# A hybrid S5, mLSTM and Conformer trunk on one core: low parts and layer-norm rows from GpSimd to VectorE

## The chip, the cores and the metric

The kernel runs on one core of a Trainium2 chip. Five engines work beside one another: TensorE (PE in the profile, PEld its weight loads), VectorE (DVE), ScalarE (ACT), GpSimd (POOL) and SyncE (SP). The time is that of one execution in device microseconds; of several runs the median is taken.

## What is computed

Four layers over 256 latent tokens and 256 context tokens, 1024 channels, in float32. Layers 0 and 3 mix tokens by an S5 state space layer, layer 1 by an mLSTM, layer 2 by a Conformer convolution. After each mixer comes a feed-forward with a 3x3 depthwise convolution on the token grid. Every sub-layer ends in a layer norm over the residual:

```python
for i in range(DEPTH):                       # 4; kinds 0, 1, 2, 0
    u = h * (1 + scale1) + shift1            # from c (latent) or c_ctx (context)
    y = mixer[kind](u)
    h = layer_norm(ALPHA * h + (1 + g1) * y, post_ln_g[i, 0], post_ln_b[i, 0])
    f = conv_ffn(h * (1 + scale2) + shift2)  # (gelu(dwconv(u @ w_gate)) * (u @ w_up)) @ w_down
    h = layer_norm(ALPHA * h + (1 + g2) * f, post_ln_g[i, 1], post_ln_b[i, 1])
# layer_norm(x, g, b) = (x - mean) * rsqrt(var + eps) * g + b; the context stream stops before the end of layer 3
```

The output is the latent stream after layer 3, whose feed-forward (the last) is computed for the latent tokens alone. FFN_HIDDEN is 2816, that is 22 units of 128 channels.

## The kernel before

**Products.** A float32 product is made of three matmuls of a 32-bit type with a shorter mantissa: each factor is split into a high part (a copy into that type) and a low part (the factor less its high part), and `mm3` (L186 to L190) issues high times high, high times low and low times high. `split` (L160) has ScalarE write the high part and `lo` (L155) subtracts: on VectorE where `e` is "V", on GpSimd where it is "G". For weights (`wload`, tile `whl`, 128 x 1024 twice) the engine is taken from `self.lo_pat`, "V" almost everywhere; ahead of the last feed-forward it is set to "VG", every second weight on GpSimd (L1859).

**Stages.** S5 (layer 0), feed-forward 0, mLSTM, feed-forward 1, Conformer, feed-forward 2 (with the context half of the last S5 layer worked into its end), the rest of that S5 layer (`s5_last`), and the last feed-forward. A feed-forward (`ffn`) makes units 0 to 11 of its hidden layer, a first part of the product with w_down, units 12 to 21, and the rest. A unit f has two weights and the products pg and pu over 512 columns (256 in the last); `ffn_act` copies pg, runs the nine taps of the depthwise convolution on it (the middle one on ScalarE, the others at L505 on VectorE), GELU, the product with pu (L520), and splits the result into `hid` with e="G" (L522). The mLSTM splits its 16 blocks `xc` with "G" for the first 15 (`self.gv`, L656).

**The join of two stages.** A stage ends with its tail products and `close`. Per token block t (0 to 3, of 128 tokens) the residual is added to z, `norm` makes the statistics (`stats`, with a power operation on GpSimd at L351) and z becomes the normed block without gain and bias. `next_x` transposes z by TensorE (tile `ut`), applies gain, bias, scale and shift by column, and splits the result into the next stage's operand X. The same z is also needed as h, by rows, for the next residual: `post` multiplies it by the row of gains and adds the row of biases, both halves of 512 columns, on GpSimd (L419, L420), and stores the result `hh` to DRAM from GpSimd's queue (L421). `close` calls it as the blocks come, and in feed-forward 2 `posts` is called from inside the S5 scan of `s5_last` for t = 2 and 3. In the last feed-forward the block t = 3 goes through `norm_out` (L353) instead, two fused instructions on VectorE, and is stored from SyncE; t = 2 is normed and posted.

**Slots.** `f5` tiles (512 columns; `gate`, `conv`, `hh`, `ytmp` and others) share a ring of 8, the large `h` slots (X, hid, the gain and bias rows of `rows`, the Conformer's hx, its diagonals `dg` and its accumulator `cvo`) a ring of 6. In the Conformer, TensorE does 12 to 15 of the 31 taps as products with diagonals that ScalarE writes (L552), and VectorE the others at L580.

The framework orders the instructions of each engine itself, by its own estimate of times, within what the data and the slots allow; what the code issues first has precedence only so far.

Of the kernel before, what the change touches and what calls it, by code (L numbers as in the profile page):

```python
# [13 lines left out]
ALU = mybir.AluOpType  # L14
# [10 lines left out]
G = 64  # L25
# [27 lines left out]
class Trunk:  # L53
    def __init__(self, ctx, tc, A, out):
        self.tc, self.nc, self.A, self.out = tc, tc.nc, A, out
        ep = lambda **k: ctx.enter_context(tc.tile_pool(**k))
        self.cp = ep(name="cp", bufs=1)
        self.wp = ep(name="wp", bufs=4)
        self.zp = ep(name="zp", bufs=4)
        self.sp = ep(name="sp", bufs=2)  # L60
        self.hp = ep(name="hp", bufs=1)
        self.dp = ep(name="dp", bufs=1, space=bass.MemoryType.DRAM)
        self.pm = ep(name="pm", bufs=4, space=bass.MemoryType.PSUM)
        self.pa = ep(name="pa", bufs=4, space=bass.MemoryType.PSUM)
        nc = self.nc
        c = self.cp.tile([P, 560], F32, name="consts")
        nc.sync.dma_start(c, A["consts"])
        self.ident = c[:, 0:128]
        self.tri = (c[:, 128:256], c[:, 256:384])
        self.foldi, self.foldf = c[0:32, 384:392], c[0:32, 392:400]  # L70
        self.diag16 = c[:, 400:416]
        self.gmask = c[:, 416:424]
        self.rep = c[:, 424:552]
        self.sgn = c[:, 552:553]
        self.dmask = c[0:8, 553:555]
        self.half = c[:, 555:556]
        self.lncol = self.cp.tile([P, 2 * DEPTH, 2, KD], F32, name="lncol")
        nc.sync.dma_start(self.lncol, A["lncol"])
        self.mods = {}
        cc = self.cp.tile([P, KD, 2], F32, name="ccin")  # L80
        nc.sync.dma_start(cc, A["cc"])
        self.cs = self.cp.tile([P, KD, 32], F32, name="cs")
        nc.vector.memset(self.cs, 0.0)
        nc.scalar.activation(self.cs[:, :, 0:2], cc, AF.Silu)
        self.fillers = deque()
        self.load = {"V": 0.0, "G": 0.0}
        self.lo_n = 0
        self.lo_pat = "V"
        self.last_w = None
        self.nxr = 3  # L90
        self.gv = 15
        self.npe = (12, 12, 12, 12, 12, 12, 14, 15)
        self.nw, self.hold = 0, None
        self.hf, self.hm, self.hcv = (4, 4), (1, 2), (2, 4)
        self.last_mm = None
        self.final = False
        self.plan = (0, 0, 0, 0, 0, 0, 0, 0, 1, 0)
        self.norm_e = "ASAS"
        self.nkb = 4
        self.nrp, self.ngt, self.nr0, self.nr1, self.nr2 = 5, 5, 4, 0, (2, 2, 0, 0)  # L100
        self.nrq = 4
        self.nlate = 2
        self.nmid = 1
        self.pre = self.mm
        self.nf0, self.nf1, self.nf2 = 2, 4, 1
# [130 lines left out]
    def close(self, tts, mms, emit, end, X=None):  # L236
        R, z, hdst, nxt = end
        if nxt and X is None:
            X = nxt["begin"]()
        pend, outs = None, []  # L240
        for t in tts:
            r = mms(t)
            if pend is not None:
                nxt["pair"](pend, z, X)
                pend = None
            emit(t, r)
            if self.final and t == 3:
                self.norm_out(R, z[t], hdst(t))
                continue
            self.norm(z[t], z[t], D, self.norm_e[t])  # L250
            outs.append(t)
            if t in (1, 3):
                if nxt:
                    pend = t // 2
            if t == 2:
                while len(outs) > (0 if self.final else 1):
                    self.post(R, z, outs.pop(0), hdst)
        if pend is not None:
            nxt["pair"](pend, z, X)
        with ExitStack() as st:  # L260
            if len(tts) == 2:
                st.enter_context(self.tc.issue_after(self.last_pow.ins))
            for t in outs:
                self.post(R, z, t, hdst)
        return X

    def mod_units(self, l, order=(1, 0, 2, 4, 3, 5), ring=("w32", W32), late=False):
        nc, A = self.nc, self.A
# [140 lines left out]
        else:  # L409
            nc.vector.tensor_tensor(out=z[t][:, hs], in0=z[t][:, hs], in1=tmp, op=ALU.add)  # L410

    def post(self, R, z, t, dst):
        nc = self.nc
        if dst(t) is None:
            return
        for half in range(2):
            hs = slice(half * 512, half * 512 + 512)
            hh = self.f5("hh")
            nc.gpsimd.tensor_tensor(out=hh, in0=z[t][:, hs], in1=R["lng"][:, hs], op=ALU.mult)  # L419
            nc.gpsimd.tensor_tensor(out=hh, in0=hh, in1=R["lnb"][:, hs], op=ALU.add)  # L420
            (nc.sync if self.final else nc.gpsimd).dma_start(dst(t)[:, hs], hh)  # L421

    def hdram(self, name):
        h = self.dp.tile([4, P, D], F32, name=name)
# [2 lines left out]
    def ffn(self, l, X, tts, hsrc, hdst, pool, nxt, mid=None):  # L427
        nc, A = self.nc, self.A
        lat = 0 not in tts
        spans = [(256, 512)] if lat else [(0, 512)]  # L430
        a0 = 256 if lat else 0
# [3 lines left out]
        z = {t: self.zt(f"z{t}") for t in tts}  # L435
        hid = {}

        def gu(fs, stag=False):
            if stag and not lat:
                outs = []  # L440
                for f in fs:
                    for j, nm in ((0, "pg"), (1, "pu")):
                        outs.append((self.mm(nm), [self.wload(A["fgu"][l, f, j])]))
                self.dense(outs, X, [(0, 256), (256, 512)])
                for i, f in enumerate(fs):
                    hid[f] = self.ffn_act(cw[:, f], outs[2 * i][0], outs[2 * i + 1][0], a0, hact)
                return
            for f in fs:
                pg, pu = self.mm("pg"), self.mm("pu")
                self.dense([(pg, [self.wload(A["fgu"][l, f, 0])])], X, spans)  # L450
                self.dense([(pu, [self.wload(A["fgu"][l, f, 1])])], X, spans)
                hid[f] = self.ffn_act(cw[:, f], pg, pu, a0, hact)
                self.fill(-(-len(self.fillers) // (NF - f)) if l == 0 else pool["fill"])

        def part(f0, f1, first, ts=tts, hook=None):
# [34 lines left out]

        def posts():
            for t in (2, 3):
                self.post(R, z, t, hdst)

        return (posts, steps), z

    def ffn_act(self, w, pg, pu, a0, hact):
        nc = self.nc
        g = self.f5("gate")
        nc.scalar.copy(g[:, a0:], pg[:, a0:])  # L500
        c = self.f5("conv")
        nc.scalar.activation(c[:, a0:], pg[:, a0:], AF.Identity, scale=w[:, 4:5], bias=w[:, 9:10])  # L502

        def tap(out, src, i):
            nc.vector.scalar_tensor_tensor(out=out, in0=src, scalar=w[:, i:i + 1], in1=out, op0=ALU.mult, op1=ALU.add)  # L505

        if a0 == 0:
            tap(c[:, 1:256], g[:, 0:255], 3)
            tap(c[:, 0:255], g[:, 1:256], 5)
        cl = c[:, 256:512].rearrange("p (r w) -> p r w", r=4)  # L510
        gl = g[:, 256:512].rearrange("p (r w) -> p r w", r=4)
        for dy in (-1, 0, 1):
            for dx in (-1, 0, 1):
                if dy == 0 and dx == 0:
                    continue
                r0, r1 = max(0, -dy), 4 - max(0, dy)
                c0, c1 = max(0, -dx), 64 - max(0, dx)
                tap(cl[:, r0:r1, c0:c1], gl[:, r0 + dy:r1 + dy, c0 + dx:c1 + dx], (dy + 1) * 3 + dx + 1)
        nc.scalar.activation(g[:, a0:], c[:, a0:], AF.Gelu_apprx_tanh)
        nc.vector.tensor_tensor(out=c[:, a0:], in0=pu[:, a0:], in1=g[:, a0:], op=ALU.mult)  # L520
        x = hact()
        self.split(c[:, a0:], x[:, 0, a0:], x[:, 1, a0:], e="G")  # L522
        return x

    def conformer(self, l, X, hsrc, hdst, pool, nxt):
# [61 lines left out]
        for i0 in range(0, KD, 1):  # L587
            dgs = diags(i0)
            outs = [(self.mm(n), [self.wload(A["cvin"][i0, j])]) for j, n in ((0, "pa"), (1, "pg"))]
            self.dense(outs, X, [(0, 256), (256, 512)] if i0 == 0 else [(0, 512)])  # L590
            late.append((i0, *glu(i0, outs[0][0], outs[1][0]), dgs))
            if i0:
                cv.append(conv(*late.pop(0)))
            self.fill(pool["cf"])
        cv.append(conv(*late.pop(0)))
        self.lo_pat = "V"
# [34 lines left out]
    def mlstm(self, l, X, hsrc, hdst, pool, nxt):  # L631
# [21 lines left out]
        def finish(i, c):  # L653
            nc.scalar.activation(c, c, AF.Silu)
            x = cact()
            self.split(c, x[:, 0], x[:, 1], e="G" if i < self.gv else "V")  # L656
            xc.append(x)
            bb = f5("bb")
            nc.scalar.activation(bb, c, AF.Copy, scale=hc[:, i, 1:2])
# [2 lines left out]
        for i in range(KE):  # L662
# [12 lines left out]
            if late:  # L675
                late.pop()()
            late.append(lambda i=i, c=c: finish(i, c))
            self.fill(pool["fill"])
        late.pop()()
        wg = self.zt("wg")[:, 0:3 * KE * 16].rearrange("p (w e n) -> p w e n", w=3, e=KE)  # L680
# [1157 lines left out]
    def run(self):  # L1838
# [17 lines left out]
        h6 = lambda t: hs[6](t) if t >= 2 else None  # L1856
        late, z = self.ffn(2, X, range(4), hs[5], h6, pool, None, lambda z: self.s5_part(prep, CTX, z))
        X, z = self.s5_last(prep, z, late, hs[6], hs[7], nx(3, 1, 6), m3[pool["m3"]:])
        self.lo_pat = "VG"  # L1859
        self.final = True  # L1860
        self.ffn(3, X, lat, hs[7], hs[8], pool, None)

# [82 lines left out]
```

## Time and profile before

| what | value |
|---|---|
| median of 3 runs | 3317.68 us (3315.51 to 3320.33) |
| profiled execution, its own time | 3317.72 us |
| span in the trace | 3315.9 us |
| mean granted clock of TensorE | 0.953 |
| busy: TensorE, VectorE, ScalarE, GpSimd | 91%, 65%, 37%, 16% |
| chain that ended last: TensorE, VectorE, DMA | 71%, 11%, 4% |

The page of the profile gives busy times of each engine, shares of the chain of work that ended last, and the costliest groups of instructions with the idle time before them. A share over the whole span hides that the stages have different limits, so the windows of one stage are read beside it: how long each engine was busy in that stretch, and the granted clock of TensorE as a share of full speed.

### The profile page before, as it was taken

The numbers are of one execution on the slowest core, as the hardware profiler recorded it, in microseconds if no ns is written. First come the engines' busy times: TensorE is split into PE (matmuls) and PEld (weight loads), VectorE is DVE, ScalarE is ACT, GpSimd is POOL, SyncE is SP. The second block draws the span as 40 slices with busy tenths as digits, with TensorE's granted clock in tenths as the row PEclk, the third lists the DMA queues.
The fourth block names the chain that finished last, engine by engine and source line by source line (L and its number), as shares of the span: only waits on it lengthen the run. The fifth ranks groups of instructions, "written<-read, shape, count | busy, mean of one in ns | idle before, by whom it ended". The sixth has DMA issues, their size and how long they took to land.

```text
span 3315.9 us, 44356 instructions
## 1 busy us (share of the span) xinstructions
PE 3013.4 (91%) x17323; PEld 2375.5 (72%) x17323; DVE 2140.8 (65%) x3489; ACT 1238.5 (37%) x2014; POOL 526.6 (16%) x456
## 2 busy tenths in 40 slices
PE   6848899998999999998889999998989999868896
PEld 4526777776777777876567778876768788656785
DVE  7795764557422223897665864667887546586988
ACT  3532432334622223333432432426534323244443
POOL 1100310004200000220000410121013101041554
PEclk9869999998999999999899999999999999988999
DMA  6623345444522223565545343223244432486352
GB/s 245 205 101 133 125 152 173 148 142 156 193 83 95 96 102 130 191 241 184 202 150 195 127 157 115 96 78 133 66 136 153 167 127 95 148 330 231 137 201 96
DMA packets 181014, 500.09 MB, mean 151 GB/s; under 512 B 18436, under 2 KB 28228, under 8 KB 177988
## 3 DMA queue, kind: packets, MB, share of 16 engines
q1 hardware_dynamic: 167748, 458.52, 40.1%
q10 hardware_dynamic: 8064, 21.96, 1.7%
q0 software_dynamic: 4992, 16.78, 1.4%
q8 instruction: 136, 2.23, 0.3%
q14 instruction: 74, 0.61, 0.1%
HBM read 443.71 MB, written 53.48 MB: 150 GB/s over the span
## 4 chain that ended last, share of the span: by engine, by line
PE 71%; DVE 11%; DMA 4%; ACT 2%; issue 2%; POOL 1%; POOLq 0%; SPq 0%; DVEq 0%; ACTq 0%
PE pg L188 4%; PE pg L189 4%; PE pg L190 4%; PE nat L189 4%; PE nat L190 4%; PE nat L188 4%; PE pu L190 4%; PE pu L189 4%; PE pu L188 4%; DVE conv L505 3%; DVE whl L155 2%; PE mlq L189 2%; PE mlk L189 2%; PE mlq L188 2%; PE mlk L188 2%
## 5 line engine op out<-in xcount | busy, mean ns | idle before, releaser
L155 DVE TENSOR_TENSOR whl<-w,whl 128x1024 fp32r<-128x1024 f32 x441 | 558.6, 1268 | 536.1 <-ACT whl L160 518.5
L160 ACT CAST whl<-w 128x1024 fp32r<-128x1024 f32 x474 | 493.7, 1048 | 817.4 <-PE nat L190 250.0
L505 DVE SCALAR_TENSOR_TENSOR conv<-gate,cw,conv 128x255 f32<-128x255 f32 (+3 forms) x836 | 402.1, 507 | 136.6 <-ACT conv L502 124.5
L188 PE MATMUL pg<-X,whl 128*128 128x512 f32 (+1 forms) x824 | 300.1, 365 | 17.8 <-DVE conv L520 15.3
L189 PE MATMUL pg<-X,whl 128*128 128x512 f32 (+1 forms) x824 | 296.1, 360 | 14.8 <-DVE X L155 14.3
L190 PE MATMUL pg<-X,whl 128*128 128x512 f32 (+1 forms) x824 | 294.7, 358 | 0.0
L188 PE MATMUL pu<-X,whl 128*128 128x512 f32 (+1 forms) x752 | 268.3, 357 | 4.3 <-DVE conv L520 3.7
L189 PE MATMUL pu<-X,whl 128*128 128x512 f32 (+1 forms) x752 | 268.2, 357 | 0.0
L190 PE MATMUL pu<-X,whl 128*128 128x512 f32 (+1 forms) x752 | 267.9, 356 | 0.0
L155 POOL TENSOR_TENSOR hid<-conv,hid 128x512 fp32r<-128x512 f32 (+1 forms) x88 | 112.9, 1284 | 939.6 <-ACT hid L160 881.8
L189 PE MATMUL nat<-whl,hid 128*128 128x512 f32 x520 | 206.7, 397 | 4.7 <-DVE whl L155 4.7
L188 PE MATMUL nat<-whl,hid 128*128 128x512 f32 x520 | 206.3, 398 | 0.0
L190 PE MATMUL nat<-whl,hid 128*128 128x512 f32 x520 | 204.9, 397 | 0.0
L188 PEld LDWEIGHTS pg<-X,whl 128*128 128x128 f32 x824 | 157.3, 191 | 54.9 <-DVE conv L520 18.1
L283 PE MATMUL mod<-w,cs 128*32 128x256 f32 x1536 | 131.2, 439 | 62.8 <-DMA w<-in_modw 62.6
L189 PEld LDWEIGHTS pg<-X,whl 128*128 128x128 f32 x824 | 156.8, 191 | 41.6 <-DVE X L155 17.2
L190 PEld LDWEIGHTS pg<-X,whl 128*128 128x128 f32 x824 | 157.3, 191 | 24.6
L351 POOL TENSOR_TENSOR mv<-mv,consts 128x1 f32<-128x1 f32 x48 | 29.4, 628 | 854.3 <-DVE mv L350 573.7
L188 PEld LDWEIGHTS pu<-X,whl 128*128 128x128 f32 x752 | 143.8, 191 | 27.3 <-DVE conv L520 3.9
L189 PEld LDWEIGHTS pu<-X,whl 128*128 128x128 f32 x752 | 143.8, 191 | 22.0
L190 PEld LDWEIGHTS pu<-X,whl 128*128 128x128 f32 x752 | 143.7, 191 | 22.0
L283 PEld LDWEIGHTS mod<-w,cs 128*32 128x32 f32 x1536 | 43.2, 117 | 126.0 <-DMA w<-in_modw 70.8
(431 smaller groups left out, 6572.7 us busy)
## 6 DMA issues: line engine op xcount, KB each, us to landing
w<-in_modw SPq DMA_DIRECT2D x192, 512.0 KB, 5.1
w<-in_fgu SPq DMA_DIRECT2D x176, 512.0 KB, 3.8
w<-in_fdn SPq DMA_DIRECT2D x98, 512.0 KB, 3.7
w<-in_glu SPq DMA_DIRECT2D x32, 512.0 KB, 4.8
w<-in_mlup SPq DMA_DIRECT2D x32, 512.0 KB, 3.8
w<-in_mlq SPq DMA_DIRECT2D x32, 512.0 KB, 3.4
w<-in_mlk SPq DMA_DIRECT2D x32, 512.0 KB, 3.5
w<-in_mlv SPq DMA_DIRECT2D x32, 512.0 KB, 3.6
```

The costliest lines, as they stand in the source:

```text
L155: (self.nc.vector if e == "V" else self.nc.gpsimd).tensor_tensor(out=out, in0=src, in1=rd(hi), op=ALU.subtract)
L160: nc.scalar.copy(hi, src)
L188: mm(ps, wh, xh, start=first, stop=False)
L189: mm(ps, wh, xl, start=False, stop=False)
L190: self.last_mm = mm(ps, wl, xh, start=False, stop=last)
L283: nc.tensor.matmul(ps[32 * q:32 * q + 32, 0:256], self.cs[:, k, :], w[:, q * 256:(q + 1) * 256], start=(k == 0), stop=(k == KD - 1), skip_ ...
L351: self.last_pow = nc.gpsimd.tensor_tensor(out=mv[:, 2:3], in0=mv[:, 1:2], in1=self.half, op=ALU.pow)
L505: nc.vector.scalar_tensor_tensor(out=out, in0=src, scalar=w[:, i:i + 1], in1=out, op0=ALU.mult, op1=ALU.add)
```

## The change

Four parts, all between GpSimd and VectorE:

- The low parts of `hid` in all feed-forwards (88, of which 66 over 512 columns) and of the 15 blocks `xc` go to VectorE, and the weights' low parts of the last feed-forward (33 of 66) too.
- `post` works one half at a time and on VectorE; the store stays on GpSimd's queue.
- `close` no longer posts. It puts the halves into a queue, `self.posts`, and the following stage takes two out after each unit, from unit 3 of a feed-forward or of the mLSTM and from block 2 of the Conformer on. z and the rows of gains and biases stay in their slots until then. The four posts inside the S5 scan stay where they are, on VectorE.
- In the last feed-forward both token blocks go through `norm_out`.

```diff
@@ close
-            if self.final and t == 3:
+            if self.final:
                 self.norm_out(R, z[t], hdst(t))
                 continue
             self.norm(z[t], z[t], D, self.norm_e[t])
...
-            if t == 2:
-                while len(outs) > (0 if self.final else 1):
-                    self.post(R, z, outs.pop(0), hdst)
         if pend is not None:
             nxt["pair"](pend, z, X)
-        with ExitStack() as st:
-            if len(tts) == 2:
-                st.enter_context(self.tc.issue_after(self.last_pow.ins))
-            for t in outs:
-                self.post(R, z, t, hdst)
+        self.posts.extend(lambda t=t, half=half: self.post(R, z, t, hdst, half) for t in outs for half in range(2) if hdst(t) is not None)
         return X
+
+    def late_posts(self, n):
+        for _ in range(min(n, len(self.posts))):
+            self.posts.popleft()()
@@ post
-            nc.gpsimd.tensor_tensor(out=hh, in0=z[t][:, hs], in1=R["lng"][:, hs], op=ALU.mult)
-            nc.gpsimd.tensor_tensor(out=hh, in0=hh, in1=R["lnb"][:, hs], op=ALU.add)
-            (nc.sync if self.final else nc.gpsimd).dma_start(dst(t)[:, hs], hh)
+    def post(self, R, z, t, dst, half):
+        V = self.nc.vector
+        hs = slice(half * 512, half * 512 + 512)
+        hh = self.f5("hh")
+        V.tensor_tensor(out=hh, in0=z[t][:, hs], in1=R["lng"][:, hs], op=ALU.mult)
+        V.tensor_tensor(out=hh, in0=hh, in1=R["lnb"][:, hs], op=ALU.add)
+        self.nc.gpsimd.dma_start(dst(t)[:, hs], hh)
@@ ffn, one unit
                 hid[f] = self.ffn_act(cw[:, f], pg, pu, a0, hact)
+                self.late_posts(2 if f > 2 else 0)
@@ ffn_act
-        self.split(c[:, a0:], x[:, 0, a0:], x[:, 1, a0:], e="G")
+        self.split(c[:, a0:], x[:, 0, a0:], x[:, 1, a0:], e="V")
@@ conformer, one block
+            self.late_posts(2 if i0 > 1 else 0)
@@ mlstm
-            self.split(c, x[:, 0], x[:, 1], e="G" if i < self.gv else "V")
+            self.split(c, x[:, 0], x[:, 1], e="V")
...
+            self.late_posts(2 if i > 2 else 0)
@@ run
-        self.lo_pat = "VG"
         self.final = True
```

GpSimd at the first join, from S5 into feed-forward 0, before (z_2729 and z_2730 are the first two token blocks, h_87 the stored rows):

```order
L351 TENSOR_TENSOR mv<-mv,consts 128x1
L419 TENSOR_TENSOR hh<-z_2729,rows 128x512 x2
L420 TENSOR_TENSOR hh<-hh,rows 128x512
L351 TENSOR_TENSOR mv<-mv,consts 128x1
L420 TENSOR_TENSOR hh<-hh,rows 128x512
L421 DMA h_87<-hh 128x512
L351 TENSOR_TENSOR mv<-mv,consts 128x1
L419 TENSOR_TENSOR hh<-z_2730,rows 128x512 x2
L421 DMA h_87<-hh 128x512
```

and now:

```order
L348 TENSOR_TENSOR mv<-mv,consts 128x1 x4
L415 DMA h_87<-hh 128x512 x8
L348 TENSOR_TENSOR mv<-mv,consts 128x1 x4
L415 DMA h_88<-hh 128x512 x6
```

The multiplies and adds are gone from between the power operations (mv), and GpSimd has the stores alone.

VectorE at the start of the Conformer, before (hm a block's gated values, hx its split, cvo the accumulator of its taps):

```order
L560 SCALAR_TENSOR_TENSOR hm<-pa,cvb,sg 128x512
L155 TENSOR_TENSOR whl<-w_17396,whl 128x1024
L155 TENSOR_TENSOR whl<-w_17402,whl 128x1024
L155 TENSOR_TENSOR hx<-hm,hx 128x512
L580 SCALAR_TENSOR_TENSOR cvo<-hm,cvw,cvo 128x2x255
L580 SCALAR_TENSOR_TENSOR cvo<-hm,cvw,cvo 128x2x254 x2
L560 SCALAR_TENSOR_TENSOR hm<-pa,cvb,sg 128x512
L580 SCALAR_TENSOR_TENSOR cvo<-hm,cvw,cvo 128x2x253 x2
L580 SCALAR_TENSOR_TENSOR cvo<-hm,cvw,cvo 128x2x252
L580 SCALAR_TENSOR_TENSOR cvo<-hm,cvw,cvo 128x2x251
L155 TENSOR_TENSOR whl<-w_17557,whl 128x1024
```

and now (z_14016 is the first token block of feed-forward 1):

```order
L155 TENSOR_TENSOR whl<-w_17541,whl 128x1024
L155 TENSOR_TENSOR hx<-hm,hx 128x512
L155 TENSOR_TENSOR whl<-w_17547,whl 128x1024
L556 SCALAR_TENSOR_TENSOR hm<-pa,cvb,sg 128x512
L413 TENSOR_TENSOR hh<-z_14016,rows 128x512 x2
L155 TENSOR_TENSOR whl<-w_17711,whl 128x1024
L414 TENSOR_TENSOR hh<-hh,rows 128x512
L155 TENSOR_TENSOR hx<-hm,hx 128x512
L414 TENSOR_TENSOR hh<-hh,rows 128x512
L576 SCALAR_TENSOR_TENSOR cvo<-hm,cvw,cvo 128x2x255 x3
L576 SCALAR_TENSOR_TENSOR cvo<-hm,cvw,cvo 128x2x254 x6
L576 SCALAR_TENSOR_TENSOR cvo<-hm,cvw,cvo 128x2x253 x6
```

The first taps stood behind the first block's hx; now they stand behind the third one's and the first half-rows of the norm, and those of three blocks come together.

VectorE in the second run of units of the last feed-forward, before:

```order
L520 TENSOR_TENSOR conv<-pu,gate 128x256
L505 SCALAR_TENSOR_TENSOR conv<-gate,cw,conv 128x4x63 x2
L505 SCALAR_TENSOR_TENSOR conv<-gate,cw,conv 128x3x63
L155 TENSOR_TENSOR whl<-w_25545,whl 128x1024
L505 SCALAR_TENSOR_TENSOR conv<-gate,cw,conv 128x192
L505 SCALAR_TENSOR_TENSOR conv<-gate,cw,conv 128x3x63 x2
L505 SCALAR_TENSOR_TENSOR conv<-gate,cw,conv 128x192
L505 SCALAR_TENSOR_TENSOR conv<-gate,cw,conv 128x3x63
L520 TENSOR_TENSOR conv<-pu,gate 128x256
```

and now:

```order
L516 TENSOR_TENSOR conv<-pu,gate 128x256
L155 TENSOR_TENSOR whl<-w_25570,whl 128x1024
L501 SCALAR_TENSOR_TENSOR conv<-gate,cw,conv 128x192
L501 SCALAR_TENSOR_TENSOR conv<-gate,cw,conv 128x4x63
L155 TENSOR_TENSOR hid<-conv,hid 128x256
L501 SCALAR_TENSOR_TENSOR conv<-gate,cw,conv 128x3x63 x3
L155 TENSOR_TENSOR whl<-w_25587,whl 128x1024
L501 SCALAR_TENSOR_TENSOR conv<-gate,cw,conv 128x192
L516 TENSOR_TENSOR conv<-pu,gate 128x256
L501 SCALAR_TENSOR_TENSOR conv<-gate,cw,conv 128x192
L155 TENSOR_TENSOR whl<-w_25604,whl 128x1024
```

Of the weights every one is now there, where it was every second, and each unit's hid has come in; taps of two units are mixed.

## Rows read from the trace of the kernel before

**Rows 1.** the page: an engine, busy us, share of span, instructions
```profile
PE 3013.4 (91%) x17323; PEld 2375.5 (72%) x17323; DVE 2140.8 (65%) x3489; ACT 1238.5 (37%) x2014; POOL 526.6 (16%) x456
```

**Rows 2.** GpSimd groups by shape: xcount, busy us, mean ns, idle
```profile
L155 POOL TENSOR_TENSOR hid<-conv,hid 128x512 fp32r<-128x512 f32 x66 | 92.2, 1399 | 875.0 <-ACT hid L160 817.2 <-issue 57.8
L155 POOL TENSOR_TENSOR whl<-w,whl 128x1024 fp32r<-128x1024 f32 x33 | 89.1, 2703 | 99.5 <-ACT whl L160 99.4
L419 POOL TENSOR_TENSOR hh<-z,rows 128x512 f32<-128x512 f32 x50 | 72.5, 1470 | 21.3 <-ACT z L375 17.0 <-ACT z L371 3.9 <-DVE z L372 0.4
L420 POOL TENSOR_TENSOR hh<-hh,rows 128x512 f32<-128x512 f32 x50 | 72.2, 1461 | 0.1
L351 POOL TENSOR_TENSOR mv<-mv,consts 128x1 f32<-128x1 f32 x48 | 29.4, 628 | 854.3 <-DVE mv L350 573.7 <-DMA hr<-in_x 253.6 <-DVE den L916 26.9
...
L155 POOL TENSOR_TENSOR xc<-xcv,xc 128x512 fp32r<-128x512 f32 x15 | 20.7, 1379 | 63.7 <-ACT xc L160 63.7
```

**Rows 3.** windows: us, busy PE, PEld, DVE, ACT, POOL, granted clock, DMA, GB/s
```profile
2062.00:2174.00 112.00, 112.00 (x482) 89.96 (x481) 71.87 (x133) 43.80 (x58) 11.61 (x9) 1.00 0.29 98
2306.00:2400.00 94.00, 93.81 (x437) 74.71 (x436) 85.56 (x129) 49.84 (x141) 0.00 (x0) 1.00 0.21 68
2400.00:2421.00 21.00, 21.00 (x106) 16.88 (x105) 13.43 (x17) 7.92 (x14) 0.00 (x0) 1.00 0.38 126
3077.80:3163.40 85.60, 73.75 (x579) 71.98 (x578) 81.28 (x110) 41.20 (x72) 47.39 (x30) 0.95 0.43 152
3199.50:3266.10 66.60, 58.01 (x482) 56.76 (x481) 62.36 (x85) 29.81 (x51) 33.29 (x17) 1.00 0.47 162
```

**Rows 4.** windows of the six joins: the second, and the sum of all six
```profile
764.00:812.00 48.00, 33.04 (x145) 25.74 (x144) 40.30 (x60) 19.29 (x32) 30.04 (x27) 0.75 0.41 151
...
sum 243.00, PE 186.53 PEld 156.04 DVE 206.89 ACT 110.45 POOL 166.29; mean PE 31.09 PEld 26.01 DVE 34.48 ACT 18.41 POOL 27.71
```

**Rows 5.** timeline of the second join, two engines: start us, us, instruction
```profile
797.79 4.77 DVE L155 TENSOR_TENSOR X<-u,X 128x256 fp32r<-128x256 f32 x2
...
799.46 2.48 POOL L420 TENSOR_TENSOR hh<-hh,rows 128x512 f32<-128x512 f32 x2
```

**Rows 6.** X as a group; tiles X, z: ns min/median/max
```profile
L155 DVE TENSOR_TENSOR X<-u,X 128x256 fp32r<-128x256 f32 x88 | 70.9, 819 | 13.1 <-ACT X L336 6.9 <-ACT X L339 5.2
...
L155 DVE TENSOR_TENSOR X<-u,X x88: 410/426/4432, 375.4 to 3086.6; 128x256 fp32r<-128x256 f32 x88
...
L372 DVE TENSOR_SCALAR z<-z,mv x12: 535/1497/1508, 369.3 to 3074.8; 128x512 f32<-128x512 f32 x12
```

**Rows 7.** waits of TensorE: us in total, times, longest
```profile
PE ut L330 <- ACT z L371: 14.6, 3, 6.8
PE pg L189 <- DVE X L155: 14.3, 9, 2.8
```

**Rows 8.** VectorE groups, window 2062:2174 (no rows on GpSimd)
```profile
L155 DVE TENSOR_TENSOR whl<-w,whl 128x1024 fp32r<-128x1024 f32 x20 | 24.4, 1220 | 4.1 <-ACT whl L160 3.6 <-DMA w<-in_fgu 0.4
...
L408 DVE SCALAR_TENSOR_TENSOR z<-hr,ytmp 128x512 f32<-128x512 f32 x4 | 2.6, 686 | 1.0 <-DMA hr<-h 1.0
```

**Rows 9.** the taps of the conformer: ns min/median/max of one
```profile
L580 DVE SCALAR_TENSOR_TENSOR cvo<-hm,cvw,cvo x139: 705/731/751, 2283.2 to 2425.3; 128x506 f32<-128x506 f32 x16, 128x502 f32<-128x502 f32 x16, 128x498 f32<-128x498 f32 x16, 128x494 f32<-128x494 f32 x16
```

**Rows 10.** timeline of the S5 scan in layer 3, GpSimd and VectorE
```profile
2943.93 5.26 POOL L419 TENSOR_TENSOR hh<-z,rows 128x512 f32<-128x512 f32 x4
...
2945.46 1.35 DVE L1273 TENSOR_TENSOR sy<-ST,apw 128x128 f32<-128x128 f32 x1
...
2954.81 0.28 DVE L1273 TENSOR_TENSOR sy<-ST,apw 128x128 f32<-128x128 f32 x1
```

**Rows 11.** groups of VectorE by shape, seven units of the last feed-forward
```profile
L505 DVE SCALAR_TENSOR_TENSOR conv<-gate,cw,conv 128x192 f32<-128x192 f32 x15 | 23.3, 1555 | 0.2
```

**Rows 12.** timeline of ScalarE ahead of the conformer
```profile
2259.84 3.90 ACT L552 ACTIVATE dg<-consts,cvws 128x128 fp32r<-128x128 f32 x13
```

**Rows 13.** DMA issues: xcount, KB each, median us from issue to landing
```profile
h<-hh POOLq DMA_DIRECT2D x48, 256.0 KB, 3.0
```

More of the change, by code (lines that the diff above doesn't have):

```diff
@@ L85, in __init__ @@
         self.fillers = deque()
+        self.posts = deque()
         self.load = {"V": 0.0, "G": 0.0}
@@ L90, in __init__ @@
         self.nxr = 3
-        self.gv = 15
         self.npe = (12, 12, 12, 12, 12, 12, 14, 15)
@@ L410, in resid @@
             nc.vector.tensor_tensor(out=z[t][:, hs], in0=z[t][:, hs], in1=tmp, op=ALU.add)
[L412 to L418, printed above, removed]
-            nc.gpsimd.tensor_tensor(out=hh, in0=z[t][:, hs], in1=R["lng"][:, hs], op=ALU.mult)
-            nc.gpsimd.tensor_tensor(out=hh, in0=hh, in1=R["lnb"][:, hs], op=ALU.add)
-            (nc.sync if self.final else nc.gpsimd).dma_start(dst(t)[:, hs], hh)
+    def post(self, R, z, t, dst, half):
[5 more added lines that the diff above has]
+        self.nc.gpsimd.dma_start(dst(t)[:, hs], hh)
     def hdram(self, name):
@@ L492, in posts @@
             for t in (2, 3):
-                self.post(R, z, t, hdst)
+                for half in range(2):
+                    self.post(R, z, t, hdst, half)
         return (posts, steps), z
```

## The prediction

> **What bounds the kernel now.** I read the busy totals first: TensorE works 91% of the span [rows 1], so a gain has to come out of its 302 idle us (3315.9 − 3013.4), and only where VectorE or GpSimd makes it wait. Next the groups of GpSimd, which price what the change touches [rows 2]: of its work, 92.2 + 89.1 + 72.5 + 72.2 + 20.7 = 347 us are low parts and the row multiply and add that move (22 narrower low parts move besides). Then three windows, to see what TensorE does beside that work. In a feed-forward of layers 0 to 2 it has no gap (112.00 of 112.00 us) while VectorE is busy 71.87: that stretch is bound by TensorE [rows 3]. In the last feed-forward it is busy 73.75 of 85.60 and 58.01 of 66.60 us, with VectorE at 81.28 and 62.36: bound by VectorE. At the six joins where one stage's layer norm feeds the next stage's first product, TensorE works 186.53 of 243.00 us and GpSimd 166.29 [rows 4]: 56.5 us of idle TensorE, beside a GpSimd that does hardly anything but the rows of the norm.
>
> What these two have to do with each other is in the timeline of one join [rows 5]: two low parts of X take VectorE 4.77 us while GpSimd's multiply and add run; over the kernel the same instruction takes 410 ns at least, 426 at the median, 4432 at worst, and 70.9 us for 88 in all where 88 × 0.426 is 37.5 [rows 6]. So VectorE's instructions with two operands in SBUF stretch until GpSimd's instruction beside them ends. TensorE waits there for just these: 14.6 us for the normed z, 14.3 us for X in front of the first products [rows 7].
>
> **The parts of the change.** The sum is made against the profiled execution, 3317.72 us (span 3315.9 and 1.8 around it); the median of the three runs, 3317.68, is the same number.
>
> *Rows at the joins, removed.* Each of the first five joins has 16 instructions of 1.47 us on GpSimd (8 halves, a multiply and an add), the sixth 8: 88 of the 100. Without them a join still holds its own chain: statistics already made, the power operation on GpSimd (0.63 us [rows 2]) with the small instructions around it, z at 0.54 us, a transpose, u, and X at 0.43 us [rows 6]; I estimate 3.4 us, for six joins 20. 56.5 − 20 = 36 us gained. As bounds: 12 if only a third of the idle time is due to GpSimd (the first rival), 45 if the chain itself shrinks to 2 us. I take 36: the stretch of the X low parts alone is 70.9 − 37.5 = 33 us, and that of the 12 halves of z up to 12 × (1.50 − 0.54) = 11 [rows 6], and these follow one another. Where the granted clock drops in a join (0.75 in the mean of the second [rows 4], so partly at the lower of its two levels, 1.2 of 2.4 GHz), a shorter gap gives back some of the slow products after it: 4 us for all six, between 0 and 8.
>
> *The same rows, added later on VectorE.* They go into units 3 to 6 of the following stage, two halves per unit, so 4 instructions of 0.69 us (the price of a two-operand instruction of that size without GpSimd [rows 8]): 2.74 us a unit. In a feed-forward a unit takes 11.2 us of TensorE (112 us for 10 units, 20 weights [rows 3, 8]) and 7.2 of VectorE; with 2.74 and the unit's own low part of 0.69 VectorE is at 10.6, below 11.2. So the first three feed-forwards pay nothing: their cover is 0.6 us a unit; if it is gone, four units cost some 1 us each, at most 4 for a stage. The 66 wide low parts and the 15 of the mLSTM [rows 2] hide in the same way, 0.69 us in a unit. The stores stay on GpSimd's queue, which now has little else: they cost no path, since the first reader of h comes a stage part later.
>
> *The conformer pays.* There VectorE is busy 85.56 of 94.00 us beside a TensorE almost without gaps, and 13.43 of the next 21 [rows 3]. Added are 16 instructions of 0.69 us, 11 us. And they hold the slot of the gain rows, of six in that ring, until they are done, so the accumulator of the taps takes a slot only when the first diagonals are used up: in the order on VectorE the taps of the first three channel blocks stand behind the third block's low part. Counted there, about 22 taps of 0.73 us [rows 9] are postponed by that, 16 us. Of these 27 us some 14 fit into what VectorE has free there (8.4 and 7.6 us, less what waits leave unusable); 13 come out at the end of the taps, on which the conformer's transposes wait. Bounds: 0 if the free time takes all of it, 27 if none. I take 12.5.
>
> *The scan of the S5 layer* (layer 3). Before, four multiplies of 5.26 us in all on GpSimd, and four adds behind them, hold VectorE's scan: the same instruction takes 1.35 us beside them and 0.28 after [rows 10]. Of 2 × 5.26 us the scan so loses 1 − 0.28/1.35, 8.3 us; now 8 instructions of 0.69, 5.5 us, stand in it. Gain 3; bounds 0 and 5.
>
> *The last feed-forward.* VectorE per unit after the change: eight taps of 189 to 252 columns, the product and the low part of hid, ten instructions that I price like X's of 256 columns, 10 × 0.43 [rows 6], and two weight low parts of 1.22 [rows 8]: 6.7 us. Before, a unit takes 85.60/12 = 7.1 us in the first run of units [rows 3], and in the second some 7.3 where it is steady, since each weight low part of 2.70 us on GpSimd [rows 2] stretches a tap beside it, to 1.56 us in the mean of one form [rows 11]. TensorE needs 58.01/10 = 5.8 [rows 3], so VectorE stays the bound. The first run of 12 units wins 12 × 0.4 to 0.6 = 5 to 7 and pays 5.5 for the 8 rows instructions that now stand in it: I take 1.5. The second, of 10 units, wins about 0.5 each: 5. The tail loses a GpSimd low part of 2.70 from its chain, and at the very end four instructions of 1.47 us on GpSimd [rows 2] no longer run beside the last norm: 2 each. Sum 10.5; bounds 4 and 18.
>
> **Sum.** −36 − 4 + 0 + 12.5 − 3 − 10.5 = −41, and 1.5 to pay in the four covered stages: −39.5, that is 3317.7 − 39.5 = 3278 us.
>
> **The rivals.**
>
> *A, the joins are their own chain.* GpSimd's rows run beside a norm whose parts follow one another anyway; only a third of the 56.5 us comes back, and the stretched instructions were not those that TensorE waited for. For it: part of TensorE's wait at joins is for ScalarE's z. Against it: 4.77 us for two X low parts of 0.43 is in the chain itself. −12 − 2 + 12.5 + 1.5 − 3 − 10.5 = −13.5: 3304 us.
>
> *B, slower: the conformer runs out of slots.* With the gain rows held through four blocks, the diagonals have one slot only: ScalarE's 24 to 32 diagonal writes of a block, 13 in 3.90 us before [rows 12], so up to 9.6 us for 32, can't start until TensorE has used up the previous block's. Exposed in each of the five blocks up to the last of the rows, that is 48 us, and with 16 for the postponed taps 64, against 52 of all gains less the cover: 3330 us. It decides once the conformer loses more than those 52. Against it: VectorE's and TensorE's orders still have three blocks in flight before the taps begin.
>
> *C, slower: stores starve.* Each store of h waits for GpSimd to hand it out; before, a store landed 3.0 us after it was issued [rows 13], with a VectorE that was itself stopped half the time. If the stores wait for pauses in a VectorE that is now busier, the 8 half-row buffers fill, and the row multiply, on VectorE, stops taps and weight low parts behind it: 24 pairs × 3.0 us = 72 us against the 39.5: 3350 us. The Trainium skill has a rule of this kind ("SBUF — State Buffer", the box on the "DVE blocks DMA" trap in it): transfers issued from GpSimd's queue have their descriptors written by GpSimd, which a VectorE instruction in a two-port mode locks out; the same page, section "Who interferes with whom", says that two-operand instructions don't enter these modes. By the first sentence the time would be that of this rival, by the second that of the forecast. The trace before has its stores at 3.0 us beside such two-operand instructions, so I give it little.
>
> *D, the change does less than it says*: the scheduler may place the postponed rows where it likes. The order shows them in the units named, so no chance of its own.
>
> **How the numbers follow.** A change under 0.2% (6.6 us) can't be told from none here. The forecast has 0.79, A 0.13, B 0.06, C 0.02. The forecast's own bounds: with most terms near their better ends, joins 45, clock 7, conformer 5, scan 4, last 14, it gives −65 (3253); with joins 28, clock 2, conformer 20, scan 0, last 6 it gives −16 (3302). With A inside, the range is 3253 to 3306. A's own spread of some 8 us reaches over the 0.2% line, so 0.05 of it counts as the same; B and C are the slower cases: faster 0.87, same 0.05, slower 0.08.
>
> **What would show it.** Right: the six joins, the same windows, with GpSimd under 1 us each and TensorE idle some 20 us in all; X low parts with a mean near 430 ns; z at 540. Feed-forwards of layers 0 to 2 as long as before per unit (11.2 us). The conformer longer by about 12 us, with TensorE idle at its end behind taps. The last feed-forward at 6.7 us a unit with VectorE over 95% busy. Wrong: the joins still idle 40 us or more with waits on ScalarE (A); waits of ScalarE's diagonals on TensorE in each block and conformer +45 (B); stores landing well over 3 us after issue (C).

## The result and the profile after

The changed kernel takes 3235.31 us (median of 4 runs, 3232.15 to 3237.21): 0.9755 of the kernel before, interval 0.9736 to 0.9773. The forecast was 3278 us, its range 3253 to 3306; the time came out 43 us below the forecast. Five other runs of it gave 0.9760 (0.9742 to 0.9778).

The page, busy time and instructions of each engine [rows 1]:

```profile
PE 2990.6 (92%) x17323; PEld 2356.8 (73%) x17323; DVE 2122.8 (66%) x3724; ACT 1238.9 (38%) x2013; POOL 168.3 (5%) x220
```

VectorE executes 235 instructions more than before and is busy 18 us less. The tiles X and z [rows 6] show why: nothing holds their instructions up any more. The three numbers are ns min/median/max:

```profile
L155 DVE TENSOR_TENSOR X<-u,X x88: 374/424/428, 365.6 to 3029.9; 128x256 fp32r<-128x256 f32 x88
...
L369 DVE TENSOR_SCALAR z<-z,mv x12: 496/542/548, 363.5 to 3022.1; 128x512 f32<-128x512 f32 x12
```

No low part of X lasts longer than 428 ns (4432 before). The waits of TensorE for these two [rows 7] fell from 14.6 and 14.3 us to:

```profile
PE ut L327 <- ACT z L368: 6.2, 3, 4.7
...
PE pg L189 <- DVE X L155: 0.6, 2, 0.4
```

To account for the 82.7 us by which the span fell, the traces were cut at the same products in both: five joins (from the last whole tail product to the end of the next stage's first run of units, to the end of the up projection in the mLSTM, to the first run of diagonals in the Conformer), the Conformer, the S5 layer of layer 3, the last feed-forward. The windows before (us, busy PE, PEld, DVE, ACT, POOL, granted clock, DMA share, GB/s; the second and the fifth join, the sum of the five, then the last feed-forward):

```profile
769.30:891.30 122.00, 107.04 (x466) 85.38 (x464) 77.68 (x99) 79.22 (x123) 51.62 (x43) 0.90 0.56 201
...
2481.30:2636.70 155.40, 148.48 (x809) 118.00 (x807) 111.30 (x186) 66.83 (x96) 42.44 (x36) 0.97 0.47 161
sum 664.50, PE 611.28 PEld 487.00 DVE 464.76 ACT 323.50 POOL 205.46; mean PE 122.26 PEld 97.40 DVE 92.95 ACT 64.70 POOL 41.09
...
3068.40:3315.90 247.50, 199.69 (x1336) 181.78 (x1336) 219.08 (x290) 104.53 (x166) 130.29 (x74) 0.94 0.41 144
```

and after, with the third join too:

```profile
754.80:863.10 108.30, 102.95 (x466) 82.74 (x464) 81.59 (x128) 78.67 (x122) 8.78 (x13) 0.97 0.64 225
1803.40:1955.80 152.40, 151.46 (x811) 122.52 (x810) 119.41 (x232) 69.49 (x100) 5.56 (x10) 1.00 0.46 155
...
2444.20:2590.90 146.70, 144.71 (x808) 114.13 (x806) 111.85 (x211) 65.65 (x96) 5.46 (x10) 1.00 0.50 171
sum 612.80, PE 593.52 PEld 473.02 DVE 455.10 ACT 319.74 POOL 28.00; mean PE 118.70 PEld 94.60 DVE 91.02 ACT 63.95 POOL 5.60
...
3015.30:3233.20 217.90, 192.13 (x1337) 178.22 (x1336) 186.85 (x355) 106.21 (x165) 5.76 (x8) 0.95 0.48 163
...
2023.00:2135.00 112.00, 112.00 (x481) 89.97 (x480) 78.09 (x142) 43.81 (x58) 0.00 (x0) 1.00 0.30 99
```

| stretch | before | after | difference |
|---|---|---|---|
| up to the first join | 363.4 | 360.2 | −3.2 (untouched; 356.2 to 363.4 over all runs) |
| five joins | 664.5 | 612.8 | −51.7: idle TensorE 53.2 to 19.3, busy 611.3 to 593.5 |
| Conformer, diagonals to tail | 196.9 | 206.0 | +9.1 |
| layer 3's S5 | 187.7 | 180.3 | −7.4 |
| last feed-forward | 247.5 | 217.9 | −29.6 |
| the rest | 1655.9 | 1656.0 | 0 |

In the last line of the fence stand ten units of feed-forward 1 [rows 3]: 112 us as before, GpSimd at 0. In the second join the same 466 products take 4.1 us less of busy time, at a granted clock of 0.97 instead of 0.90 (means between the two levels, 1.2 and 2.4 GHz). The window of the fourth join holds 264 products after and 271 before, and the Conformer's behind it 898 and 892, so one to two us of these two differences are the cut. Over the other four joins, with the same products in both to within one, idle time falls by 30.2 us (40.2 to 10.0) and busy time by 14.3 (564.5 to 550.2). By the trace's record of the granted clock, TensorE was busy at the lower level for 39.9 us in these four before and for 8.0 after; half of the 31.9 us would be lost at half the clock, an estimate of 15.9 us beside the 14.3 measured. So the clock accounts for the shorter busy time.

### The profile page after: what moved, and what is told of

Same layout as the page of the kernel before. It is cut to its first block, busy times and chain, and to the rows that moved or that the text cites. A ratio compares the mean times of both kernels' runs of the same rounds, so it can differ in the third digit from the quotient of the medians.

```text
span 3233.2 us, 44254 instructions
## 1 busy us (share of the span) xinstructions
PE 2990.6 (92%) x17323; PEld 2356.8 (73%) x17323; DVE 2122.8 (66%) x3724; ACT 1238.9 (38%) x2013; POOL 168.3 (5%) x220
## 4 chain that ended last, share of the span: by engine, by line
PE 79%; DVE 6%; DMA 4%; ACT 1%; issue 1%; POOL 0%; SPq 0%; DVEq 0%; ACTq 0%; POOLq 0%
PE pg L188 5%; PE pg L189 5%; PE pg L190 5%; PE nat L189 5%; PE nat L190 5%; PE nat L188 5%; PE pu L188 4%; PE pu L189 4%; PE pu L190 4%; PE mlq L189 2%; PE mlq L190 2%; PE mlk L190 2%; PE mlk L189 2%; PE mlk L188 2%; PE mlq L188 2%; PE v L188 2%
## 5 line engine op out<-in xcount | busy, mean ns | idle before, releaser
L155 DVE TENSOR_TENSOR whl<-w,whl 128x1024 fp32r<-128x1024 f32 x474 | 578.7, 1223 | 523.3 <-ACT whl L160 507.9
L501 DVE SCALAR_TENSOR_TENSOR conv<-gate,cw,conv 128x255 f32<-128x255 f32 (+3 forms) x836 | 341.6, 437 | 77.1 <-ACT conv L498 67.4
L188 PE MATMUL nat<-whl,hid 128*128 128x512 f32 x520 | 206.0, 398 | 0.0
L188 PEld LDWEIGHTS nat<-whl,hid 128*128 128x128 f32 x520 | 98.0, 189 | 24.2 <-issue 0.8
```

Of the source, the lines that this page charges most:

```text
L155: (self.nc.vector if e == "V" else self.nc.gpsimd).tensor_tensor(out=out, in0=src, in1=rd(hi), op=ALU.subtract)
L188: mm(ps, wh, xh, start=first, stop=False)
```

## The experiments

The theory to start with: a VectorE instruction with two operands in SBUF lasts as long as GpSimd's beside it, so each part gains where it stood. Ratios are to the kernel before, run beside each kernel.

**The parts alone.** Kernel before with three edits:

```diff
-        self.split(c[:, a0:], x[:, 0, a0:], x[:, 1, a0:], e="G")
+        self.split(c[:, a0:], x[:, 0, a0:], x[:, 1, a0:], e="V")
-            self.split(c, x[:, 0], x[:, 1], e="G" if i < self.gv else "V")
+            self.split(c, x[:, 0], x[:, 1], e="V")
-        self.lo_pat = "VG"
```

> The kernel before with the low parts alone moved to VectorE (hid, xc, the weights of the last feed-forward); rows of the norm stay on GpSimd at the stage ends. Theory 1: a VectorE instruction with two operands in SBUF lasts as long as the GpSimd instruction beside it, so each part gains by itself in the stage where it stood; the low parts carry most of the 30 us that the last feed-forward (247.5 to 218 us) lost. Expected 3290 us (3282 to 3298), joins and Conformer as before. Rival: in the last feed-forward VectorE has no room for 33 more weights, and the 30 us came from the rows and the last norm: 3308 us or more.

0.9922 (0.9904 to 0.9939), 3286.3 us. The other half, the changed kernel with these three lines as they were before:

> The changed kernel with all low parts back on GpSimd: rows of the norm on VectorE within the following stage, and the last norm fused, alone. Theory 1: five joins shorter by 52 us in all, Conformer longer by 9, the S5 scan shorter by 7, in units 3 to 6 some stretch of the rows by hid on GpSimd (4): 3319 - 46 = 3273 us (3264 to 3280). Rival: joins need both parts, since hid and xc low parts on GpSimd beside the first units hold VectorE there too: 3290 us or more.

0.9844 (0.9820 to 0.9868), 3259.6 us. The gains add up: 0.78% and 1.56% against 2.45% together, and both rivals fall. The joins are the rows' alone: cut at the same products, the five take 665 us with the low parts alone, as before the change, and 613 with the rows alone. The last feed-forward, with the low parts alone:

```profile
3064.60:3283.50 218.90, 191.46 (x1336) 176.54 (x1336) 188.29 (x344) 106.88 (x166) 23.21 (x20) 0.96 0.48 162
```

and with the rows alone:

```profile
3013.40:3259.30 245.90, 201.48 (x1337) 184.37 (x1336) 214.37 (x301) 103.47 (x165) 112.37 (x62) 0.93 0.44 145
```

28.6 of its 29.6 us are the low parts'.

**Which low parts, and by what rule.** The changed kernel with one line:

```diff
+        self.lo_pat = "VG"
         self.final = True
```

> The changed kernel with every second weight of the last feed-forward back on GpSimd. Theory 1: 33 x 2.7 = 89 us of GpSimd stretch VectorE by some 60 us where it saves 40, and the last feed-forward is bound by VectorE as a whole, not unit by unit: +20, 3255 us (3248 to 3262). By the per-unit price of the prediction (7.1 to 7.3 against 6.7 us a unit, 22 units): +10, 3245 us. Rival that the weights don't matter: 3237 us.

0.9822 (0.9801 to 0.9843), 3253.0 us, within the range of theory 1. Its last feed-forward, 23.7 us longer than the changed kernel's:

```profile
3006.60:3248.20 241.60, 199.68 (x1336) 182.89 (x1336) 213.17 (x323) 103.44 (x165) 89.78 (x40) 0.94 0.44 147
```

With "VVVG" in that line:

> The changed kernel with every fourth weight of the last feed-forward on GpSimd instead of none. Theory 1 (VectorE bounds this stage as a whole, so each GpSimd weight costs what it stretches less what it saves): half of the 22 us that every second one cost: +9 to +12, 3246 us. Rival (a unit has slack for one of the kind, only pairs collide): within 3 us of 3235; rival (any of them on the chain costs all): 3255 us.

0.9769 (0.9744 to 0.9794), 3240.7 us, and in the profiled execution the stage is only 1.7 us longer than the changed kernel's. That execution took 3228.9 us, the other three 3239.6 to 3242.0, so the stage may be longer in those; by the medians the whole is some 4 us longer than the changed kernel, with intervals that overlap. Theory 1 asked for 9 to 12. With the low parts of hid alone on GpSimd there (`e="G" if a0 else "V"`):

> The changed kernel with the 22 low parts of hid of the last feed-forward back on GpSimd. Threshold theory (after the change TensorE bounds this stage and VectorE has some 30 us to spare in it, as every fourth weight on GpSimd showed): 0 to +3, 3236 us (3232 to 3239). Linear theory (what GpSimd stretches less what it saves, at the rate of the weights): +6 or more, 3241 us or more.

0.9744 (0.9725 to 0.9763), 3231.6 us, just under the threshold theory's range, and the stage 2.7 us shorter than the changed kernel's: this part of the change gained nothing. The same window with every fourth weight, and with hid, on GpSimd:

```profile
3007.50:3227.10 219.60, 194.49 (x1337) 180.26 (x1336) 197.49 (x339) 104.40 (x165) 45.54 (x24) 0.95 0.48 162
```

```profile
3018.00:3233.20 215.20, 193.08 (x1336) 179.20 (x1336) 188.89 (x333) 105.39 (x165) 39.47 (x30) 0.94 0.49 165
```

So the cost isn't linear. With VectorE busy 187 to 197 us the stage takes 215 to 220; with 213 to 219 it takes 242 to 248. What TensorE waits for in this stage shows which engine sets it (us in total, times, longest); before:

```profile
PE pg L188 <- DVE conv L520: 15.3, 11, 1.6
```

after:

```profile
PE pu L188 <- DVE conv L516: 4.4, 1, 4.4
```

Before, TensorE waited for VectorE's product in unit after unit; after, once. Where between 197 and 213 us the stage turns is not measured, and GpSimd's busy time parts the same runs (at most 46 us in the short ones, at least 90 in the long ones): that VectorE's total is the right measure, and not GpSimd's, is argued, not shown.

**The place or the engine.** The rows on VectorE, but issued at the end of `close` (before, those of the first two blocks came already at the third):

```diff
-        self.posts.extend(lambda t=t, half=half: self.post(R, z, t, hdst, half) for t in outs for half in range(2) if hdst(t) is not None)
+        for t in outs:
+            for half in range(2):
+                if hdst(t) is not None:
+                    self.post(R, z, t, hdst, half)
```

> The changed kernel with the rows of the norm on VectorE, but issued at the end of the stage as before, not within the next. Theory 1 (the engine matters): 16 instructions of 0.69 us stand in VectorE's queue at a join, part of them in its idle time; joins +4 each, Conformer 9 shorter since its slots are free early: 3245 us (3235 to 3258). Rival (the place matters): joins as long as before the change, 3235 + 52 - 9 = 3278 us.

0.9855 (0.9834 to 0.9876), 3264.6 us: far from the theory's 3245, and short of the rival's 3278. Then the rows at the late place, computed on GpSimd (`V = self.nc.gpsimd` in `post`):

> The changed kernel with the rows of the norm at their late place but computed on GpSimd. Theory 1 (what counts is what VectorE has to do beside them): in units of the feed-forwards and the mLSTM VectorE has 3 to 4 us free per unit, which hides the stretch, so the five joins stay as short as in the changed kernel; the Conformer, where VectorE is full, loses some 12 more, the S5 scan its 7 again, the first units of the last feed-forward 3: 3235 + 22 = 3257 us (3248 to 3266). Rival (only the engine counts): the joins' 52 us come back in full: 3285 us or more. Other rival (only the place counts): 3235 us.

0.9802 (0.9777 to 0.9827), 3253.9 us, in the range of theory 1; the profiled execution was the fastest of its four, 3244.6 us. The five joins in the first and in the second of these:

```profile
sum 647.50, PE 601.37 PEld 478.38 DVE 465.20 ACT 320.84 POOL 36.20; mean PE 120.27 PEld 95.68 DVE 93.04 ACT 64.17 POOL 7.24
```

```profile
sum 614.70, PE 593.55 PEld 473.57 DVE 468.22 ACT 309.55 POOL 124.56; mean PE 118.71 PEld 94.71 DVE 93.64 ACT 61.91 POOL 24.91
```

Another engine at the old place wins 17 of the 51.7 us, the late place with the old engine 49.8. With the rows on VectorE at the end of `close`, nothing stretches the low parts of X any more (the three numbers are ns min/median/max):

```profile
L155 DVE TENSOR_TENSOR X<-u,X x88: 373/419/428, 367.4 to 3062.3; 128x256 fp32r<-128x256 f32 x88
```

Still the joins are 34.7 us longer than the changed kernel's, two thirds of the 51.7: the rows themselves, 11 us of VectorE a join, now stand there. At the joins the place decides: the next stage's unit has VectorE time to hide the rows in, stretched or not, and the join has none. At the late place the engine counts for a few us: in the profiled execution with GpSimd the rest of the S5 layer takes 185.2 us against 180.3, the last feed-forward 222.2 against 217.9, and the Conformer 2.6 us more, where 12 were expected.

**What a longer join costs.** Eight extra instructions per join, results not used:

```diff
         if pend is not None:
+            if len(tts) == 4:
+                d = self.f5("dly")
+                for _ in range(8):
+                    self.nc.vector.tensor_scalar(out=d, in0=z[3][:, 512:1024], scalar1=1.0, scalar2=None, op0=ALU.mult)
             nxt["pair"](pend, z, X)
```

> The changed kernel with eight extra one-operand VectorE instructions of some 0.5 us, whose result is not used, in front of the last X of each of the first five joins. Clock theory (a longer join costs its idle time and, on top, a lower granted clock in the products after it): TensorE idle +12 to +20 over the five joins and TensorE busy +5 to +12 there, 3257 us (3250 to 3266). Rival (the joins' busy time fell for another reason, the order of the products): idle as above, busy unchanged within 2 us: 3250 us or less.

0.9758 (0.9733 to 0.9784), 3237.0 us: nothing, and the joins are as long as the changed kernel's to within about 1 us each. In the order they stand between the low parts of X; that what they displaced was on nobody's path is argued from that. Both forecasts missed, and the clock stays untested by it. So a chain that X needs, sixteen in place on z:

```diff
+                for _ in range(16):
+                    self.nc.vector.tensor_scalar(out=z[3][:, 512:], in0=z[3][:, 512:], scalar1=1.0, scalar2=None, op0=ALU.mult)
```

> The changed kernel with a chain of sixteen extra VectorE instructions of 0.42 us on the last token block's z (times one, in place) ahead of its transposes, at the first five joins: 6.7 us a join that nothing can hide. Clock theory: TensorE idle +6 per join, and the products after it run partly at the lower clock again, half as much as the idle time as in the kernel before (33.9 us idle and 17.8 us busy): 3235 + 34 + 15 = 3284 us (3276 to 3292), granted clock of these windows down. Rival (busy time doesn't depend on the gap): idle alone, 3268 us (3262 to 3272).

0.9802 (0.9782 to 0.9823), 3252.7 us; the second, third and fifth join and the sum of the five:

```profile
757.60:866.80 109.20, 103.08 (x466) 82.69 (x464) 87.36 (x144) 77.56 (x123) 10.70 (x13) 0.97 0.65 224
1810.90:1966.80 155.90, 152.97 (x811) 122.83 (x810) 125.16 (x248) 69.54 (x100) 5.56 (x10) 1.00 0.44 151
...
2455.40:2607.80 152.40, 147.10 (x809) 115.59 (x807) 118.29 (x227) 66.22 (x96) 5.46 (x10) 0.99 0.48 165
sum 630.00, PE 603.02 PEld 477.88 DVE 482.76 ACT 320.78 POOL 29.96; mean PE 120.60 PEld 95.58 DVE 96.55 ACT 64.16 POOL 5.99
```

Of 80 × 0.42 = 33.6 us on VectorE 17.2 reach the joins, so half is hidden, against both forecasts. In the four joins with equal products it is 13.0, of which 7.4 idle TensorE and 5.6 longer busy time (550.2 to 555.8), in the fifth join 144.71 to 147.10 at 0.99 instead of 1.00. So a join that opens costs more than its idle time, here some three quarters as much again. But the clock is the smaller part of that: TensorE was busy at the lower level for 11.2 us in these four joins, 8.0 in the changed kernel, which by the estimate above is 1.6 of the 5.6 us, and the third join grew by 1.5 us of busy time at 1.00 in both. What made the rest is open.

**The Conformer.** All eight half-rows after the first block:

```diff
-            self.late_posts(2 if i0 > 1 else 0)
+            self.late_posts(8 if i0 == 0 else 0)
```

> The changed kernel with all eight half-rows of the join before the Conformer released after its first channel block instead of two after each of blocks 2 to 5. Slot theory: VectorE's 15 us of idle time at the Conformer's start come from the gain rows holding the slot of the taps' accumulator; with it free early the Conformer (+9 us) comes down to +2 to +4: 3230 us (3226 to 3233). Rival (the work of 11 us alone): no change, 3235 us, or slower since the eight stand ahead of hx.

0.9731 (0.9706 to 0.9756), 3228.1 us. In the changed kernel the accumulator's edges are set when the first diagonals have been used (start, us, instruction, idle before and what ended it), and the Conformer's end waits for the taps:

```profile
2258.58 0.32 POOL L571 MEMSET cvo<- 128x2 f32 x8 [57.89 <-PE cps L190]
```

```profile
2378.00:2405.00 27.00, 15.34 (x83) 10.15 (x82) 19.50 (x48) 11.71 (x17) 2.66 (x4) 0.68 0.50 165
```

Released early, they are set as soon as the last store of rows is issued:

```profile
2246.67 0.33 POOL L571 MEMSET cvo<- 128x2 f32 x8
```

From the first diagonal product to the last product ahead of the fifth join, before, in the changed kernel, and with the early rows:

```profile
2282.28:2481.26 198.98, 191.78 (x901) 153.30 (x900) 168.92 (x270) 95.31 (x222) 4.33 (x7) 0.97 0.28 95
```

```profile
2236.38:2444.15 207.77, 194.84 (x906) 154.42 (x905) 173.90 (x286) 96.29 (x227) 8.75 (x22) 0.96 0.31 103
```

```profile
2237.26:2436.25 198.99, 192.60 (x906) 153.32 (x905) 173.91 (x282) 96.50 (x227) 8.28 (x22) 0.99 0.33 111
```

The Conformer is back at its old length with VectorE as busy as in the changed kernel, so the work need cost nothing. What went is VectorE's wait ahead of the taps: the first tap starts 11.4 us after the first diagonal product instead of 25.0. That this wait was for the slot is shown by the edges; but the edit also moves the rows out of the blocks where VectorE is full (6 of their 16 instructions now stand ahead of the first diagonal product), and no run keeps them late with the slot free.

The same, with the rows in the S5 scan moved behind it (`posts()` after `s5_sa` instead of ahead of `lat[3]()`):

> The version with the early rows in the Conformer, and the four half-rows of feed-forward 2 moved from inside the S5 scan to behind it (where VectorE has weights alone). If the 5.5 us of rows lengthen the scan, the S5 stage is 4 to 5 us shorter: 3224 us (3219 to 3228), 11 below the changed kernel. Rival (in the scan they stood in VectorE's waits): as the version before, 3228 us.

0.9735 (0.9717 to 0.9754), 3229.0 us. From the second part product of feed-forward 2 to the end of the S5 layer it takes 423.9 us, against 424.1 in the version before it: the rows in the scan stood in VectorE's waits. Beside it the changed kernel again:

> The changed kernel itself again, beside the other three on the same chip: 3235 us, 0.9755 of the kernel before.

0.9760 (0.9742 to 0.9778), 3237.1 us (3233.6 to 3239.3), against 3225.1 to 3231.5 for the version with the early rows and the moved scan rows: it beats both kernels, the changed one by 8 us (median to median, no run of the one within those of the other), and the windows lay the gain to the early rows.

## Why the prediction was wrong

The sign and the places held; the gains of the joins' clock, of the last feed-forward and of the S5 scan were set too small.

- *Joins, idle time* (−36 for six): five gave 33.9, the sixth nothing, its window up to the first unit being 9.4 us before and 9.5 after. The size is right, the reason half of it: the prediction laid it to GpSimd's stretch, but without any stretch the rows at the old place leave 34.7 of the 51.7 us. It takes both that GpSimd leaves the join and that the rows' work does.
- *Joins, clock* ("4 us for all six, between 0 and 8"): 14.3 us less busy time in four of them for the same products. This is the first failed step: the term was set without a row for what the products behind a gap cost, though the windows held it (0.75 in the second). The record of the clock accounts for it (15.9 us estimated). The chain of sixteen shows longer busy time too, though mostly for another reason than the clock.
- *Last feed-forward* ("so VectorE stays the bound", −10.5 and the sixth join): −29.6. This is the second failed step. The prices of a unit were right, as its groups in the stage show:

```profile
L155 DVE TENSOR_TENSOR whl<-w,whl 128x1024 fp32r<-128x1024 f32 x63 | 76.8, 1221 | 10.1 <-ACT whl L160 9.6
L501 DVE SCALAR_TENSOR_TENSOR conv<-gate,cw,conv 128x189 f32<-128x189 f32 x88 | 34.1, 411 | 5.1 <-ACT conv L498 4.9
```

  But a stage isn't bound unit by unit. In the second run of units after the change TensorE has no gap, where it was busy 58.01 of 66.60 us before [rows 3], and it fits 27 more products in:

```profile
3134.30:3196.70 62.40, 62.40 (x509) 61.17 (x508) 59.42 (x118) 36.17 (x58) 0.00 (x0) 1.00 0.59 195
```

  VectorE is busy 59.42 us there, less than the 67 that ten units cost at 6.7, so part of its work for them stands outside, beside the products with w_down. Over the whole stage VectorE went from 219.1 busy of 247.5 to 186.9, and its waits no longer hold TensorE, as the two lines of waits above show: TensorE became the bound. Every fourth weight back on GpSimd costs the profiled stage 1.7 us, every second 23.7.
- *S5 scan* (−3): −7.4. The 5.5 us of rows that were set against the gain stood in waits; moving them out changed nothing (423.9 against 424.1).
- *Conformer* (+12.5): +9.1, about one of it by the cut. The late taps are as the prediction said; the part charged to work need not cost anything, as the early rows show. Rival B, its larger form, fell.
- *Cover in the steady units* (+1.5): 0 or near it. Units without rows take 112.00 us as before [rows 3], and in the third join, whose window holds units 3 to 6 with the rows, TensorE is busy 151.46 of 152.40 us.
- *Rival A* fell with TensorE's idle time in the joins at 19.3 of 53.2 us. Its sum took −12, a third of 36; a third of the 56.5 us that it names is 19, and the rival would have stood at 3297 us. *Rival C* fell: the stores land in 2.6 us, 3.0 before [rows 13].

```profile
h<-hh POOLq DMA_DIRECT2D x48, 256.0 KB, 2.6
```

The Trainium skill ("SBUF — State Buffer", section "Who interferes with whom") says that `tensor_tensor` has no two-port mode and, as an inference, that it leaves GpSimd's descriptor writing alone; the trace agrees, with 96 more of them on VectorE for these rows and stores that land in 2.6 us.

The untouched start gave 3.2 us by chance of the run.

## What to carry to other kernels

Price an engine's relief over the whole stage in which its work can move, not per unit: take its busy time there, take away what the other engine stretches it by and add what is moved in, and compare with the other engine's; then look who waits for whom. Work that only has to be done some time belongs out of the join and into a unit with room; there it matters little on which engine it runs, but a slot that it keeps can cost more than its work. And a gap in TensorE's work costs more than its idle time: read the busy time and the granted clock behind it too.

## What was not expected of the hardware

VectorE took on 235 instructions and was busy 18 us less (2140.8 to 2122.8). The moved work is some 170 us of it after the change (rows 63.3, low parts of hid 54.7, weights 40.3, xc 10.3), so nearly 190 us of stretch fell away, an estimate by difference. The instruction with one operand in SBUF, z at L369, was stretched by GpSimd like those with two: 1497 ns at the median before, 542 after.

A VectorE instruction can be held by several GpSimd instructions in a row. The longest low part of X (4432 ns [rows 6]) is the first of the two that start at 797.79 [rows 5]. It began 0.45 us ahead of GpSimd's multiply and ended at 802.23, 0.29 us behind the last of three GpSimd instructions:

```profile
798.24 1.27 POOL L419 TENSOR_TENSOR hh<-z,rows 128x512 f32<-128x512 f32 x1
799.46 2.48 POOL L420 TENSOR_TENSOR hh<-hh,rows 128x512 f32<-128x512 f32 x2
```

Half of a 6.7 us chain on VectorE at a join was hidden, against the expectation. At the first join eleven of its sixteen instructions stand, from 370.39 us on, between low parts of X that don't read that half of z; only the last five follow one another, ahead of the four low parts that do:

```profile
379.06 2.27 DVE L258 TENSOR_SCALAR z<-z 128x512 f32<-128x512 f32 x5
```
